# V turned in 32x32 blocks by VectorE ahead of its store, instead of by TensorE in each head

## The chip, the core and the metric

One core of a Trainium2 chip runs the whole program once. The engines are TensorE (PE, with its weight loads PEld), VectorE (DVE), ScalarE (ACT), GpSimd (POOL) and SyncE (SP); SP, ACT and POOL also issue DMAs. The metric is the device time of one execution in microseconds (us); lower is better. Arithmetic is in float32, and most products are made of three matmuls (high part by high part and the two cross terms) on operands split into a high and a low part.

## The reference

One decoder layer over 1024 tokens of width 2048. An RMS norm of the input goes into one projection with 8192 columns: queries, keys, values and gates of 8 stick-breaking heads (head width 128) and 8 differential heads (two q/k pairs of width 64, values of 128). Cut to what matters here:

```
hn = rmsnorm(h, norm_mix_g)
sb_q, sb_k, sb_v, sb_g, df_q, df_k, df_v, df_g = split(hn @ w_in)
sb_out = stick_breaking_attention(sb_q, sb_k, sb_v)          # w @ v, tokens contracted
df_out = rmsnorm(differential_attention(rope(df_q), rope(df_k), df_v, lam), subln_g) * (1 - lambda_init)
mixed  = concat(sb_out * silu(sb_g), df_out * silu(df_g))
h = h + mixed @ w_out
h = h + sigmoid(rmsnorm(h, norm_ple_g) @ w_ple_gate) * (p @ w_ple_proj)
out = rmsnorm(h, norm_final_g)
```

## The kernel before

All activations are kept transposed: features on the 128 partitions, tokens along the free axis. The 1024 tokens are two halves of 512; half 1 comes first in the attention. A tile is mostly 128x512.

The program has four stages.

**1. V and gates (to about 620 us).** The columns of values and gates are computed with a seven-product scheme on 2x2 blocks (the products are called A11, A12, S1, S2, S3, S4 and A22 after their operand). Class `Seven` runs it: `prod` writes the twelve matmuls of one product and then calls `step`, which is one *slot*: it splits one weight operand for later products (`whigh` on ACT, `wlow` on DVE, with the differences T1 to T4 on DVE), runs what `soon` holds for this slot, and takes from the queue `xq`. A *unit* u (0 to 15) is one head's V and gate. In phase 0 a unit is S2, A22 of the unit before, S1, S4 of the unit before, S3; in phase 1 it is A11, A22 of the unit before, S2, S4 of the unit before, A12, S1, S3. An opening computes A11 and A12 of phase 0 for all units first (`outer` and `evict` for units 0 to 7, a loop for 8 to 15). Results leave PSUM through DVE (`u2`, `u3`, sums into the tiles `hc`) or, where nothing is to be added, through an ACT copy (`evict`, and `second_result` for A12), and `vput` stores them to `vg_d`, with addition in DRAM after the first. S2 and S3 accumulate in one PSUM bank b: A22 of the same unit adds to it after S3, so `u3` (b + s1) must have read it before; the line is L1255. Four tiles with the tag "f" take the outgoing results in turn.

**2. Heads (about 620 to 1650 us).** For each half and each of 16 heads (the differential ones first), `unit` writes the 192 matmuls of the q and k projection, and between every three matmuls `side.tick()` runs what is due of the attention of the head before: tables of tick numbers (`SVG`, `VGD`, `SBT`, `TT`, ...) give the place of each step. `load_vg` loads the head's V and gate (tiles `vf`, `gf`) on SP, `normed` multiplies them by the tokens' RMS factor `rstd`, and `values` turns V: four TensorE transposes of 128x128 into the PSUM tile `vps`, since the product with the attention weights contracts tokens; then ACT casts the high part and DVE makes the low part.

```
vps = pp.tile([P, 4, P], F32, name="vps", tag="t")
for j in range(4):
    T.transpose(vps[:, j, :], vg[0][:, j * P:(j + 1) * P], ident)
```

**3. Output projection (about 1660 to 1985 us)**, again by `Seven` (`op`), 8 units in 2 phases. In phase 1 `sums` forms row combinations of the new h for the next stage, in two steps `one` and `two` put on `soon` in following slots. `u3` stands there too (L1912). **4. The embedding gate (from about 1985 us)**, 8 units, by `gprod`; `gate_loads` issues the loads of an operand and puts its splits on `xq` some slots on; `plew` (L1851) casts the embedding weights, `ple` multiplies with them.

The order of PE, DVE and ACT is that of the code: each runs its instructions in the order in which they are written, and every wait is a semaphore. POOL's and SP's orders follow from the planner. DMAs on SP are issued in order.

Of the kernel before, what the change touches and what calls it, by code (L numbers as in the profile page):

```python
# [13 lines left out]
F32 = mybir.dt.float32  # L14
# [3 lines left out]
ALU = mybir.AluOpType  # L18
AX = mybir.AxisListType

P = 128
# [4 lines left out]
H = 8  # L26
# [13 lines left out]
LV = ((2.5, 2.5), (1, 2))  # L40
# [30 lines left out]
def _body(ctx, nc, tc, ap):  # L71
    PSUM = bass.MemoryType.PSUM
    const = ctx.enter_context(tc.tile_pool(name="const", bufs=1))
# [20 lines left out]
    G.memset(eps5, SUB_EPS)  # L94
    lsum = const.tile([P, 2], F32, name="lsum", tag="lsum")
    lam = const.tile([P, 1], F32, name="lam", tag="lam")
    qzs = {}
    nqz = [0]

# [206 lines left out]
        G.dma_start(S4, t, accum_op=ALU.add)  # L306


    def attention(at, pz, half, hd, q, qz, K, KL, VV, sg, vg, state):

        sb = hd < H
# [143 lines left out]
        def values():  # L455

            assert "v" in state
            vps = pp.tile([P, 4, P], F32, name="vps", tag="t")
            for j in range(4):
                T.transpose(vps[:, j, :], vg[0][:, j * P:(j + 1) * P], ident)  # L460
            v = at.tile([P, 2, 4, P], F32R, name="v", tag="v")
            side.later(1 if sb else LV[half][0], lambda: A.copy(v[:, 0], vps))

            def low():
                V.tensor_tensor(v[:, 1], vps, v[:, 0].bitcast(F32), op=ALU.subtract)
                VV.insert(0, v)
                if half == 1:
                    G.dma_start(v_d[hd], v.rearrange("p a b c -> p (a b c)"))

            side.later(2 if sb else LV[half][1], low)  # L470

        def turn(pr, g):

# [149 lines left out]
    with tc.tile_pool(name="at", bufs=2) as at, ExitStack() as banks:  # L623
# [26 lines left out]
        def ftile():  # L650
            return ev.tile([P, HALF], F32, name="hc", tag="f", bufs=4)
# [254 lines left out]
        def combined(i):  # L906
# [25 lines left out]

            return {nm: partial(part, nm) for nm in ("S1", "S2", "S3", "S4", "A22")}

        def vput(o, ph, hf, blk, u):
            G.dma_start(vg_d[hf, blk, u], o, **(dict(accum_op=ALU.add) if ph else {}))  # L936

# [267 lines left out]
        for u in range(H, 2 * H, 2):  # L1205
            pair = []
            for nm in ("A11", "A12"):
                for j in range(2):
                    if nm == "A11":
                        pair.append(pp.tile([P, HALF], F32, name="pa", tag="acc", bufs=2))  # L1210
                    prod(u + j, 0, nm, pair[j], nm == "A11")
                    o = ftile()
                    A.copy(o, pair[j])
                    if nm == "A11":
                        G.dma_start(vgpart_d[u + j], o)
                    else:
                        vput(o, 0, 1, 0, u + j)
        prev = None
        for ph in range(2):
            for u in range(2 * H):  # L1220
# [74 lines left out]
                consts_late()  # L1295

        side.add([(4, norms)])
        X0 = {}

        early = {}  # L1300
# [59 lines left out]
        def gate_operand(nm, i, eng):  # L1360

            hi, lo = op.places(GPLACE[nm][i], "g" + nm)
            src = {"A11": h_d[1, i], "A12": h_d[1, i + 8], "A22": h_d[0, i + 8]}.get(nm)
            if src is None:
                src = hcomb_d[SUMS.index(nm), i]
            gain = {"A11": i, "A12": i + 8, "A22": i + 8, "S3": i}.get(nm)
            if gain is not None:
                gain = gvec[:, 1, gain:gain + 1]
            if nm == "A12":
                with tc.issue_after(op.loaded.ins):  # L1370
                    eng.dma_start(lo.bitcast(F32), src)
# [116 lines left out]
        for half in (1, 0):  # L1488
# [5 lines left out]
            for hd in (ORDER0, ORDER1)[half]:  # L1494
# [10 lines left out]
                def load_vg(vg=vg, hd=hd, half=half):  # L1505
                    for i in range(2):
                        vg.append(f32t(("vf", "gf")[i]) if hd < H else ev.tile([P, HALF], F32, name=("vf", "gf")[i], tag="xt", bufs=4))
                        with tc.issue_after(lastw[0].ins):
                            nc.sync.dma_start(vg[i], vg_d[half, i, hd])
# [49 lines left out]
                if sb:  # L1559
# [18 lines left out]
                    def normed(i, vg=vg, rstd=rstd, state=state):  # L1578
                        V.tensor_tensor(vg[i], vg[i], rstd, op=ALU.mult)
# [8 lines left out]
                else:  # L1588
# [19 lines left out]
                    def turned(c, fs=fs):  # L1608
                        f, sw = [t.bitcast(F32) for t in fs[c]]
                        V.tensor_tensor(sw, sw, cs[:, 1, :], op=ALU.mult)  # L1610
                        V.tensor_tensor(f, f, sw, op=ALU.add)
# [24 lines left out]
                        if c:  # L1636
                            store_k()

                    def normed(i, vg=vg, rstd=rstd, state=state):
                        V.tensor_tensor(vg[i], vg[i], rstd, op=ALU.mult)  # L1640
# [166 lines left out]
        def rest_of(st_, first):  # L1807

            u, ph, b, c, s1, u2, hq = st_
            nm, o_, t, hf, ch = ("A22", b, s1, 0, u) if first else ("S4", c, u2, 1, u + 8)  # L1810
            prod(u, ph, nm, o_, False)
            o = ftile()
            V.tensor_tensor(o, o_, t, op=ALU.add)
            put(o, ph, hf, ch)
            if ph == 1:
                hrows[u, hf] = o
                if not first:
                    lag = {6: 10, 7: 7}.get(u, 1)
                    op.soon.extend((op.slot + lag + i, fn) for i, fn in enumerate(sums(u, hq, hrows.pop((u, 0)), hrows.pop((u, 1)))))

        praws = []

# [599 lines left out]
```

## Time and profile before

| | us |
|---|---|
| median of three runs (2359.6 to 2361.01) | 2360.39 |
| the profiled execution | 2361.19 |
| its span, first to last instruction | 2359.4 |
| PE busy in the span | 2317.2 |
| DVE busy | 1789.8 |
| ACT busy | 1189.0 |

The profile is of one execution. A group's row gives busy time and the mean of one instruction; a wait's row gives who waited for whom, in total, how often and the longest. A row of the timeline gives start, length, engine, line, operation, output and input. Line numbers (L460) are those of the kernel before.

### The profile page before, as it was taken

What the parts mean: (1) busy time and instruction counts of PE and PEld (TensorE: products, weight loads), DVE (VectorE), ACT (ScalarE), POOL (GpSimd) and SP (SyncE); (2) the same over time, 40 slices, a digit from 0 to 9 for tenths busy, and PEclk for the clock granted to TensorE, in tenths of its full rate; (3) what the DMA queues carried; (4) which work ended last, traced back from release to release, by engine and by line L of the source; (5) the groups of instructions that cost most, each with busy time, mean ns of one, the idle gap of its engine ahead of it and who ended that gap; (6) DMA issues with size and microseconds to landing.
All of it is one profiled execution on the core that took longest, in us unless ns stands there. A gap on an engine that the chain in (4) does not pass through costs nothing.

```text
span 2359.4 us, 32445 instructions
## 1 busy us (share of the span) xinstructions
PE 2317.2 (98%) x11096; PEld 1928.3 (82%) x11096; DVE 1789.8 (76%) x3123; ACT 1189.0 (50%) x2214; POOL 327.3 (14%) x480
## 2 busy tenths in 40 slices
PE   9999999999999999999999999999999999999997
PEld 7888888888888878887888888888878878788886
DVE  7489676666677787777888876767887877788778
ACT  6334243333367775445676764445633435533544
POOL 2211112332200000000001011011121232000000
PEclk9999999999999999999999999999999999999998
DMA  7699589999977788787656566677888778898666
GB/s 260 225 313 344 170 255 281 293 278 271 303 246 252 246 266 299 256 263 245 204 182 199 165 190 215 203 214 238 213 211 215 242 229 269 291 326 292 243 227 217
DMA packets 252725, 581.02 MB, mean 246 GB/s; under 512 B 28496, under 2 KB 41040, under 8 KB 252560
## 3 DMA queue, kind: packets, MB, share of 16 engines
q1 hardware_dynamic: 177952, 394.34, 49.7%
q0 software_dynamic: 55312, 149.71, 24.2%
q10 hardware_dynamic: 19296, 34.90, 4.3%
q8 instruction: 87, 1.43, 0.3%
q14 instruction: 78, 0.64, 0.1%
HBM read 373.32 MB, written 213.91 MB: 249 GB/s over the span
## 4 chain that ended last, share of the span: by engine, by line
PE 71%; DVE 12%; ACT 7%; DMA 6%; issue 3%; SPq 0%; ACTq 0%; DVEq 0%
PE acc L263 7%; PE acc L261 7%; PE acc L262 7%; PE pbc L708 6%; PE pbc L710 6%; PE pbc L709 6%; PE pa L708 2%; PE pa L710 2%; PE pa L709 2%; PE tp L480 2%; DMA wraw<-w_out 2%; PE pb L708 1%; PE pb L710 1%; PE pb L709 1%; PE pb L1941 1%
## 5 line engine op out<-in xcount | busy, mean ns | idle before, releaser
L799 ACT CAST wpr<-T 128x512 fp32r<-128x512 f32 x208 | 125.3, 621 | 440.3 <-DVE T L764 360.4
L261 PE MATMUL acc<-xh,whi 128*128 128x512 f32 x768 | 315.0, 410 | 0.0
L263 PE MATMUL acc<-xh,wlo 128*128 128x512 f32 x768 | 302.5, 394 | 1.5 <-DMA wlo<-wlo_d 1.4
L262 PE MATMUL acc<-xl,whi 128*128 128x512 f32 x768 | 301.0, 392 | 0.0
L263 PEld LDWEIGHTS acc<-xh,wlo 128*128 128x128 f32 x768 | 144.5, 188 | 36.2 <-DMA wlo<-wlo_d 3.6
L262 PEld LDWEIGHTS acc<-xl,whi 128*128 128x128 f32 x768 | 145.4, 189 | 24.0
L261 PEld LDWEIGHTS acc<-xh,whi 128*128 128x128 f32 x768 | 145.0, 189 | 23.4 <-DVE qk L1567 0.2
L799 ACT CAST wpr<-wraw 128x512 fp32r<-128x512 f32 x144 | 88.6, 618 | 146.9 <-DMA wraw<-w_vg 40.2
L813 DVE TENSOR_TENSOR wpr<-T,wpr 128x512 fp32r<-128x512 f32 x208 | 145.8, 701 | 9.2 <-ACT wpr L799 6.8
L936 POOL DMA_DIRECT2D vg_d<-hc x120 | 86.8, 724 | 328.4 <-DVE hc L1181 187.9
L503 DVE TENSOR_TENSOR awl<-tp,awh 128x256 fp32r<-128x256 f32 (+1 forms) x160 | 92.5, 578 | 42.8 <-ACT awh L498 42.2
L498 ACT CAST awh<-tp 128x256 fp32r<-128x256 f32 (+1 forms) x160 | 80.6, 504 | 82.6 <-PE tp L480 76.3
L813 DVE TENSOR_TENSOR wpr<-wraw,wpr 128x512 fp32r<-128x512 f32 x144 | 97.7, 686 | 23.5 <-ACT wpr L799 23.5
L321 DVE CUSTOM_DVE_ANT_0 z<-z,masks 128x512 f32<-128x512 f32 (+7 forms) x128 | 97.1, 769 | 23.0 <-PE z L341 14.0
L708 PE MATMUL pbc<-cS,wpr 128*128 128x512 f32 x288 | 112.0, 389 | 0.0
L709 PE MATMUL pbc<-cS,wpr 128*128 128x512 f32 x288 | 112.0, 389 | 0.0
L710 PE MATMUL pbc<-cS,wpr 128*128 128x512 f32 x288 | 112.0, 389 | 0.0
L373 DVE TENSOR_TENSOR_SCAN st<-pt 128x511 f32<-128x511 f32 (+3 forms) x64 | 86.7, 1354 | 27.2 <-ACT pt L366 26.8
L366 ACT ACTIVATE pt<-z 128x512 f32<-128x512 f32 (+3 forms) x64 | 41.8, 653 | 76.6 <-DVE z L349 74.6
L528 PE MATMUL av<-awl,v 128*128 128x256 f32 x256 | 73.4, 287 | 1.7 <-DVE awl L503 1.7
L526 PE MATMUL av<-awh,v 128*128 128x256 f32 x256 | 72.0, 281 | 0.7 <-ACT awh L498 0.7
L527 PE MATMUL av<-awh,v 128*128 128x256 f32 x256 | 72.2, 282 | 0.0
(589 smaller groups left out, 6816.5 us busy)
## 6 DMA issues: line engine op xcount, KB each, us to landing
wlo<-wlo_d SPq DMA_DIRECT2D x94, 512.0 KB, 5.2
whi<-whi_d SPq DMA_DIRECT2D x74, 512.0 KB, 4.1
wraw<-w_vg SPq DMA_DIRECT2D x129, 256.0 KB, 4.8
vg_d<-hc POOLq DMA_DIRECT2D x120, 256.0 KB, 5.7
wraw<-w_in SPq DMA_DIRECT2D x54, 512.0 KB, 5.3
wraw<-w_gate SPq DMA_DIRECT2D x92, 256.0 KB, 4.9
wraw<-w_out SPq DMA_DIRECT2D x72, 256.0 KB, 4.6
wlo_d<-wlo SPq DMA_DIRECT2D x34, 512.0 KB, 3.4
```

Source lines behind the costliest of these rows:

```text
L261: T.matmul(acc[c], hi[:, k2, kh, c, :], xh, start=first, stop=False)
L262: T.matmul(acc[c], hi[:, k2, kh, c, :], xl, start=False, stop=False)
L263: T.matmul(acc[c], lo[:, k2, kh, c, :], xh, start=False, stop=last)
L321: V.tensor_tensor_reduce(z, z, mwide[:, 0:n], -DF_SCALE, 3.0e38, ALU.add, ALU.min, mx)
L373: V.tensor_tensor_scan(st[:, off + 1:nkey], pt[:, off:nkey - 1], pt[:, off:nkey - 1], initial=1.0, op0=ALU.mult, op1=ALU.bypass)
L503: V.tensor_tensor(wl[:, o, :], tp[:, o, :], wh[:, o, :].bitcast(F32), op=ALU.subtract)
L708: T.matmul(o, wh[:, w], xh, start=start and k == 0, stop=False, skip_group_check=True)
L709: T.matmul(o, wh[:, w], xl, start=False, stop=False, skip_group_check=True)
L710: T.matmul(o, wl[:, w], xh, start=False, stop=k == 3, skip_group_check=True)
L799: A.copy(t[:, 0], src)
L813: V.tensor_tensor(t[:, 1], src, t[:, 0].bitcast(F32), op=ALU.subtract)
L936: G.dma_start(vg_d[hf, blk, u], o, **(dict(accum_op=ALU.add) if ph else {}))
```

## The change

V is turned before it is stored. VectorE's transpose works on blocks of 32x32: `vturn` turns the sixteen blocks of each 128-token group of a 128x512 tile and writes them sorted by the place of the 32 tokens in their group of 128. Each head's load then puts the blocks where they belong: four DMAs, one for each 32 partitions, gather runs of 128 elements from the four partition groups. The head's V thus arrives with tokens on the partitions.

```
+    def blocks(t):
+        return t.rearrange("p (b k j) -> p b k j", b=4, k=4)
...
+        def vturn(o, src):
+            V.transpose(blocks(o).rearrange("p b k j -> p k b j"), blocks(src))
...
         def values():
-            vps = pp.tile([P, 4, P], F32, name="vps", tag="t")
-            for j in range(4):
-                T.transpose(vps[:, j, :], vg[0][:, j * P:(j + 1) * P], ident)
             v = at.tile([P, 2, 4, P], F32R, name="v", tag="v")
-            side.later(1 if sb else LV[half][0], lambda: A.copy(v[:, 0], vps))
+            hi, lo = [v[:, i].rearrange("p k (b j) -> p b k j", b=4) for i in range(2)]
+            raw = blocks(vg[0])
+            A.copy(hi, raw)
             def low():
-                V.tensor_tensor(v[:, 1], vps, v[:, 0].bitcast(F32), op=ALU.subtract)
+                V.tensor_tensor(lo, raw, hi.bitcast(F32), op=ALU.subtract)
...
-            side.later(2 if sb else LV[half][1], low)
+            side.later(1, low)
...
         def evict(n, u):
-            if u in (3, 5) and n == 3:
+            if n > 3:
+                vturn(o, aa[u])
+            elif u in (3, 5):
...
         def rest_of(st_, first):
             V.tensor_tensor(o, o_, t, op=ALU.add)
-            vput(o, ph, hf, blk, u)
+            if not first:
+                return vput(o, ph, hf, blk, u)
+            def turned():
+                v = ftile()
+                vturn(v, o)
+                vput(v, ph, hf, blk, u)
+            if ph == 1 and u == 2 * H - 1:
+                turned()
+            else:
+                gv.soon.append((gv.slot + 2, turned))
...
                 def second_result():
                     prod(u, ph, "A12", a, False)
                     o = ftile()
-                    A.copy(o, a)
+                    vturn(o, a)
...
+        def columns(hf):
+            ps = pp.tile([P, 4, P], F32, name="rps", tag="t")
+            for j in range(4):
+                T.transpose(ps[:, j, :], rstds[hf][:, j * P:(j + 1) * P], ident)
+            side.later(1, lambda: A.copy(rcol[:, hf, :], ps[:, :, 0]))
+        side.add([(20, partial(columns, 1)), (24, partial(columns, 0))])
...
-                            nc.sync.dma_start(vg[i], vg_d[half, i, hd])
+                            if i:
+                                nc.sync.dma_start(vg[i], vg_d[half, i, hd])
+                            for a in range(0 if i else 4):
+                                rows = slice(32 * a, 32 * a + 32)
+                                nc.sync.dma_start(vg[i][rows].rearrange("p (b e) -> p b e", b=4), vg_d[half, i, hd].rearrange("(b p) (a e) -> a p b e", b=4, a=4)[a])
```

The loop of the opening for units 8 to 15 gets `vturn` in place of the ACT copy at A12 in the same way. Since tokens are now on the partitions, `normed` multiplies V by a factor per partition and token group: `columns` turns the two rows of factors once into `rcol`, with eight TensorE transposes in the first head. Two places of the later stages move:

```
-        e = [(op.slot + (3 if nm in ("A11", "A12") else 2), gate_operand(nm, i0 + j, eng)) for j in range(n)]
+        e = [(op.slot + (3 if nm in ("A11", "A12") or eng is A and (nm, i0) == ("S2", 0) else 2), gate_operand(nm, i0 + j, eng)) for j in range(n)]
...
-                    op.soon.extend((op.slot + lag + i, fn) for i, fn in enumerate(sums(...)))
+                    op.soon.extend((op.slot + lag + (1 + (lag == 1)) * i, fn) for i, fn in enumerate(sums(...)))
```

What stands in the queues, at three places. On DVE, the end of the first unit of phase 1 in the V stage, before (wpr is a weight operand, T a difference of weight blocks, hc a result on its way out):

```order
L1236 TENSOR_TENSOR u_2895<-pbc,s_2826 128x512
L813 TENSOR_TENSOR wpr<-T_2782,wpr 128x512
L1181 TENSOR_TENSOR hc<-pbc,u_2716 128x512
L813 TENSOR_TENSOR wpr<-wraw,wpr 128x512
L690 TENSOR_TENSOR cS4l<-cS4l,cS4h 128x512 x2
L764 TENSOR_TENSOR T_2961<-wraw 128x512
L764 TENSOR_TENSOR T_2964<-wraw,T_2961 128x512
L813 TENSOR_TENSOR wpr<-wraw,wpr 128x512
L690 TENSOR_TENSOR cS4l<-cS4l,cS4h 128x512 x2
L1255 TENSOR_TENSOR u_2973<-pbc,s_2826 128x512
```

and the same piece now:

```order
L1256 TENSOR_TENSOR u_2925<-pbc,s_2857 128x512
L816 TENSOR_TENSOR wpr<-T_2810,wpr 128x512
L939 STREAM_TRANSPOSE hc<-hc 128x4x4x32
L1189 TENSOR_TENSOR hc<-pbc,u_2745 128x512
L816 TENSOR_TENSOR wpr<-wraw,wpr 128x512
L693 TENSOR_TENSOR cS4l<-cS4l,cS4h 128x512 x2
L939 STREAM_TRANSPOSE hc<-pa 128x4x4x32
L767 TENSOR_TENSOR T_2994<-wraw 128x512
L767 TENSOR_TENSOR T_2997<-wraw,T_2994 128x512
L816 TENSOR_TENSOR wpr<-wraw,wpr 128x512
L693 TENSOR_TENSOR cS4l<-cS4l,cS4h 128x512 x2
L1275 TENSOR_TENSOR u_3006<-pbc,s_2857 128x512
```

Two block transposes have come in ahead of u3 (L1255, now L1275): that of the A22 result two slots earlier, and that of A12, which reads its bank. On PE, in the second head of half 1, before:

```order
L263 MATMUL acc_5697<-xh_5159,wlo 128x512
L460 MATMUL vps<-ident,vf 128x128 x4
L261 MATMUL acc_5697<-xh_5162,whi 128x512
L262 MATMUL acc_5697<-xl_5163,whi 128x512
L263 MATMUL acc_5697<-xh_5162,wlo 128x512
```

and now:

```order
L264 MATMUL acc_5775<-xh_5222,wlo 128x512
L262 MATMUL acc_5775<-xh_5225,whi 128x512
L263 MATMUL acc_5775<-xl_5226,whi 128x512
L264 MATMUL acc_5775<-xh_5225,wlo 128x512
L262 MATMUL acc_5776<-xh_5216,whi 128x512
```

The four transposes are gone and nothing stands in their place. On DVE in phase 1 of the output projection, before (hq and hc are rows of the new h, hr the old ones):

```order
L1798 SCALAR_TENSOR_TENSOR hq<-hq,gneg 128x512
L1800 SCALAR_TENSOR_TENSOR hc<-hc,gneg,hq 128x512
L1912 TENSOR_TENSOR u_17915<-pbc,s_17780 128x512
L813 TENSOR_TENSOR wpr<-T_17906,wpr 128x512
L1914 TENSOR_TENSOR u_17915<-u_17915,hr 128x512
L1919 TENSOR_TENSOR hq<-pbc,u_17915 128x512
```

and now:

```order
L1952 TENSOR_TENSOR u_17924<-pbc,s_17793 128x512
L816 TENSOR_TENSOR wpr<-T_17919,wpr 128x512
L1838 SCALAR_TENSOR_TENSOR hq<-hq,gneg 128x512
L1840 SCALAR_TENSOR_TENSOR hc<-hc,gneg,hq 128x512
L1954 TENSOR_TENSOR u_17924<-u_17924,hr 128x512
L1959 TENSOR_TENSOR hq<-pbc,u_17924 128x512
```

The two combinations stand behind u3 and the weight remainder, in six of the eight units. In the gate stage the casts of the first four S2 operands on ACT stand behind one more cast of `plew`, one weight cast and one sigmoid.

More of the change, by code (lines that the diff above doesn't have):

```diff
@@ L96, in _body @@
     lam = const.tile([P, 1], F32, name="lam", tag="lam")
+    rcol = const.tile([P, 2, 4], F32, name="rcol", tag="rcol")
     qzs = {}
@@ L1212, in _body @@
                     o = ftile()
-                    A.copy(o, pair[j])
                     if nm == "A11":
+                        A.copy(o, pair[j])
                         G.dma_start(vgpart_d[u + j], o)
                     else:
+                        vturn(o, pair[j])
                         vput(o, 0, 1, 0, u + j)
@@ L1576, in taken, with normed @@
                         side.later(2, low)
-                    def normed(i, vg=vg, rstd=rstd, state=state):
-                        V.tensor_tensor(vg[i], vg[i], rstd, op=ALU.mult)
+                    def normed(i, vg=vg, rstd=rstd, state=state, half=half):
+                        if i:
+                            V.tensor_tensor(vg[i], vg[i], rstd, op=ALU.mult)
+                        else:
+                            r = rcol[:, half, :].rearrange("p (b k j) -> p b k j", b=1, j=1)
+                            V.tensor_tensor(blocks(vg[i]), blocks(vg[i]), r.broadcast_to([P, 4, 4, 32]), op=ALU.mult)
                         state.add("v")
@@ L1637, in spread, with normed @@
                             store_k()
-                    def normed(i, vg=vg, rstd=rstd, state=state):
-                        V.tensor_tensor(vg[i], vg[i], rstd, op=ALU.mult)
+                    def normed(i, vg=vg, rstd=rstd, state=state, half=half):
+                        if i:
+                            V.tensor_tensor(vg[i], vg[i], rstd, op=ALU.mult)
+                        else:
+                            r = rcol[:, half, :].rearrange("p (b k j) -> p b k j", b=1, j=1)
+                            V.tensor_tensor(blocks(vg[i]), blocks(vg[i]), r.broadcast_to([P, 4, 4, 32]), op=ALU.mult)
                         state.add("v")
@@ L1818, in rest_of @@
                     lag = {6: 10, 7: 7}.get(u, 1)
-                    op.soon.extend((op.slot + lag + i, fn) for i, fn in enumerate(sums(u, hq, hrows.pop((u, 0)), hrows.pop((u, 1)))))
+                    op.soon.extend((op.slot + lag + (1 + (lag == 1)) * i, fn) for i, fn in enumerate(sums(u, hq, hrows.pop((u, 0)), hrows.pop((u, 1)))))
         praws = []
```

## The prediction

> **What bounds the kernel now.** I read the page's engine shares first, then the time by stage, then who waits for whom on TensorE (PE), then single steps in the timeline.
>
> ```profile
> PE 2317.2 (98%) x11096; PEld 1928.3 (82%) x11096; DVE 1789.8 (76%) x3123; ACT 1189.0 (50%) x2214; POOL 327.3 (14%) x480
> ```
>
> PE is busy for 2317.2 of 2359.4 us: only 42 us are without a matmul. Whatever leaves PE's queue is gained unless another engine then holds PE up. The stages (start:end, length, busy us of PE, PEld, DVE, ACT, POOL, granted clock, DMA share, GB/s):
>
> ```profile
> 103.64:198.84 95.20, 95.20 (x421) 78.83 (x420) 83.89 (x135) 36.04 (x63) 20.04 (x37) 1.00 0.92 314
> 198.84:226.36 27.52, 27.52 (x123) 22.77 (x122) 26.03 (x42) 12.50 (x22) 2.74 (x6) 1.00 0.99 358
> 226.36:294.04 67.68, 67.68 (x300) 56.05 (x299) 48.27 (x79) 19.16 (x32) 8.69 (x16) 1.00 0.56 182
> 294.04:329.52 35.48, 35.32 (x156) 28.90 (x154) 29.05 (x46) 17.56 (x31) 4.15 (x7) 1.00 0.70 220
> 329.52:610.80 281.28, 280.53 (x1237) 232.28 (x1238) 185.00 (x268) 102.00 (x160) 86.30 (x121) 1.00 1.00 283
> ...
> 640.00:900.00 260.00, 254.22 (x1267) 211.60 (x1266) 201.48 (x490) 179.98 (x418) 16.85 (x29) 1.00 0.75 255
> 900.00:1200.00 300.00, 293.56 (x1490) 246.66 (x1490) 232.09 (x438) 165.18 (x325) 20.32 (x31) 0.99 0.73 244
> ```
>
> The first five rows are the V and gate stage (the first four its phase 0, the fifth its phase 1): PE has no gap, DVE is at 88%, 95%, 71%, 82% and 66%, ACT at half or less. The last two are heads of attention: PE 98%, DVE 77%. The clock is full throughout. PE's waits (us in total, times, longest):
>
> ```profile
> PE pbc L708 <- DVE u L1912: 3.5, 4, 1.5
> ...
> PE z L1859 <- ACT pwhl L1851: 1.5, 1, 1.5
> ...
> PE pbc L708 <- DVE u L1255: 0.9, 1, 0.9
> ```
>
> None is a wait for the V transposes. They cost PE its own time.
>
> **PE loses 128 transposes (values).** The timeline at one group (start, length):
>
> ```profile
> 656.87 0.39 PE L262 MATMUL acc<-xl,whi 128*128 128x512 f32 x1
> 657.10 0.39 PE L263 MATMUL acc<-xh,wlo 128*128 128x512 f32 x1
> 657.33 0.60 PE L460 MATMUL vps<-ident,vf 128*128 128x128 f32 x4
> 657.69 0.48 PE L261 MATMUL acc<-xh,whi 128*128 128x512 f32 x1
> 658.00 0.40 PE L262 MATMUL acc<-xl,whi 128*128 128x512 f32 x1
> ...
> L460 PE MATMUL vps<-ident,vf 128*128 128x128 f32 x128 | 19.2, 272 | 0.0
> ```
>
> A matmul of 512 columns starts every 0.23 us. Without the four, L261 would start at 657.33 and L262 at 657.56; it starts at 658.00. So a group costs 0.44 us, and 32 groups 14.1 us, all on the path. The 272 ns of the last row is the time through the array, not what one takes from the queue (four end after 0.60).
>
> [...]
>
> Added: two groups of four (columns), 0.9 us. They stand at ticks 20 and 24 of the first head; the rotary table reads one half's factors at tick 20 too, so they are made by then, and I see no wait.
>
> **DVE gains 64 block transposes.** 32 replace ACT copies (16 in the opening, 16 at A12 of phase 1), 32 come on top (A22: one per unit in both phases). No such operation is in the trace. The nearest row is the lane shuffle of the same tile from PSUM:
>
> ```profile
> L1606 DVE STREAM_SHUFFLE sw<-acc 128x512 f32<-128x512 f32 x32 | 23.6, 736 | 0.0
> L373 DVE TENSOR_TENSOR_SCAN st<-pt 128x511 f32<-128x511 f32 (+3 forms) x64 | 86.7, 1354 | 27.2 <-ACT pt L366 26.8
> ```
>
> I take 0.74 us (the scan's 1.35 is the upper end), 47 us in all. A unit of phase 0 is five products of twelve matmuls, 13.6 us (95.2 / 7): 83.89 + 7 x 0.74 = 89.1 of 95.2 in the first seven units, 26.03 + 1.5 = 27.5 of 27.5 in the next two, then slack again. Phase 1 has 185.0 + 30 x 0.74 = 207 of 281. What PE would wait for is u3, read from the bank before A22 may add to it:
>
> ```profile
> 198.84 0.69 DVE L1255 TENSOR_TENSOR u<-pb,s 128x512 f32<-128x512 f32 x1 [0.81 <-PE pb L710]
> 213.21 0.68 DVE L1255 TENSOR_TENSOR u<-pbc,s 128x512 f32<-128x512 f32 x1
> 226.36 0.68 DVE L1255 TENSOR_TENSOR u<-pbc,s 128x512 f32<-128x512 f32 x1
> ...
> 329.52 0.69 DVE L1255 TENSOR_TENSOR u<-pbc,s 128x512 f32<-128x512 f32 x1
> ...
> 330.27 0.50 PE L708 MATMUL pbc<-cA,wpr 128*128 128x512 f32 x1 [0.90 <-DVE u L1255]
> ```
>
> At 198.84 it starts as S3 ends. The next S3 ends at 212.44, so u3 at 213.21 is 0.77 late; at 226.36, 0.32. One transpose more per unit makes that about 1.5 and 1.8. PE follows u3's start by 0.75 (329.52 to 330.27), and A22 is due one product (13.6 / 5 = 2.72) after S3's end: 1.8 + 0.75 = 2.55, just no stall. At 330 there is none to spare: 0.90 is waited already, and up to three transposes come into that stretch, 0 to 2.2 us. I take +1.5 for the stage (0 to 5, the upper end with 1.35 a piece).
>
> [...]
>
> The ring of four output tiles is filled once more per unit, and the turned A22 tile is stored two products later, so POOL's stores change order. A tile is free once its store has landed:
>
> ```profile
> vg_d<-hc POOLq DMA_DIRECT2D x120, 256.0 KB, 5.7
> ```
>
> Four fills in 13.6 us leave each tile more than twice that; cost 0, and up to 1 in the opening, where stores and products share the ring (inside the 5 above).
>
> ACT loses 32 copies, where it idles. The V cast and its remainder keep their counts and are no longer behind PE; they stand a row or two earlier, and K's remainder then comes after them. That, and the V factor by column, I put at 0 (under 0.7 of DVE, hidden by PE's products).
>
> **V's load is four DMAs of 512 B pieces, not one of 2 KB rows.** On the SP queue:
>
> ```profile
> L1509 SPq DMA_DIRECT2D vf<-vg_d x32: 319/424/1072, 632.2 to 1628.3; - x32
> ...
>   DMA vf<-vg_d: 0.2, 1
> ...
> L1845 SPq DMA_DIRECT2D pw<-w_pp x32: 545/556/953, 1990.4 to 2305.6; - x32
> ...
> vf<-vg_d SPq DMA_DIRECT2D x32, 256.0 KB, 5.7
> ...
> pw<-w_pp SPq DMA_DIRECT2D x32, 128.0 KB, 4.8
> ...
> 877.71 0.77 SPq L1509 DMA_DIRECT2D vf<-vg_d  x1
> ...
> 884.04 0.69 DVE L1579 TENSOR_TENSOR vf<-vf,ssa 128x512 f32<-128x512 f32 x1 [0.19 <-DMA vf<-vg_d]
> ```
>
> The pw load is the nearest: 512 B pieces, 256 of them, land 4.8 us after an issue of 0.56. Four issues of 0.42 to 0.56 put the last piece 1.3 to 1.7 later and its landing at about 6.1 to 6.5 instead of 5.7. The gate load and the next weights are that much later on SP (96 more issues in all). DVE waits for V once in 32 heads, 0.2 us: at 884.04, 6.3 us after the issue, in a stick-breaking head of the first half run. Those eight heads have 4 ticks from load to use, all others 6 to 19.5. There DVE, and behind it the gate factor, the weight remainders and the scan, may wait 0.3 to 0.8 a head, some 4 us; with DVE at 77% I take a third, 1.2, on PE (0 to 4).
>
> **Row combinations later (output stage).** Before:
>
> ```profile
> 1918.10 0.39 PE L708 MATMUL pa<-cA11h,wpr 128*128 128x512 f32 x1
> 1918.15 0.74 DVE L1798 SCALAR_TENSOR_TENSOR hq<-hq,gneg 128x512 f32<-128x512 f32 x1
> 1918.93 0.75 DVE L1800 SCALAR_TENSOR_TENSOR hc<-hc,gneg,hq 128x512 f32<-128x512 f32 x1
> 1919.60 0.69 DVE L1912 TENSOR_TENSOR u<-pbc,s 128x512 f32<-128x512 f32 x1
> 1920.34 0.50 PE L708 MATMUL pbc<-cA,wpr 128*128 128x512 f32 x1 [1.40 <-DVE u L1912]
> ```
>
> The two go behind u3, which then starts 1.45 earlier. The four waits (3.5, and 0.16 each of modelled tail over the 0.23 step, 4.1) go but for some 0.3. Next in line is the weight chain of that unit, so I take -3.0 (0 to -4.1).
>
> **S2 splits a slot later.** ACT's two casts no longer stand ahead of pwhl:
>
> ```profile
> 2028.77 1.27 ACT L684 CAST cgS<-cgS 128x512 fp32r<-128x512 f32 x2 [0.93 <-DMA cgS<-hcomb_d]
> 2029.94 0.40 ACT L1851 CAST pwhl<-pw 128x256 fp32r<-128x256 f32 x1
> 2030.40 0.50 PE L1859 MATMUL z<-ph,pwhl 128*128 128x512 f32 x1 [1.49 <-ACT pwhl L1851]
> ```
>
> That frees pwhl by two casts and the 0.93: -1.5 (0 to -1.65).
>
> **Sum.** The profiled execution took 2361.19 us (0.80 above the median of the three). 2361.2 - 14.1 + 0.9 + 1.5 + 1.2 - 3.0 - 1.5 = 2346.2. The bounds: 2361.2 - 14.1 + 0.9 - 4.1 - 1.65 = 2342 and, with nothing gained late, 2361.2 - 13.2 + 5 + 4 = 2357, not all at once.
>
> **Rivals.**
> - *Block transposes far dearer (slower).* Phase 0 has 226 - 187 = 39 us of idle DVE for its 16, 2.4 each, phase 1 96 for 32, 3.0 each. Beyond that each us lands on PE: at 3.5 us, 16 x 1.1 + 32 x 0.5 = 34, so 2380; it ends slower from about 3.1 us. The shuffle and the scan speak against it. 0.03.
> - *DVE late for u3 in each unit of phase 0* (the transpose waits for tiles still being stored, or costs 1.3): 16 x 0.5 + 2 more, 2354. For it, the 95% in two units; against it, the 12% that DVE idles in the seven before and 29% in the five behind. 0.10.
> - *V comes late in both halves:* 2 us of DVE in 16 heads, a quarter on PE, 8 us: 2353. For it, four issues on a queue that carries every weight; against it, 6 to 19.5 ticks of lead and the one wait of 0.2. 0.07.
> - *Heads paced by DVE and ACT, not PE:* the 14 us turn into waits, about 2358. DVE at 77% and only some 12 us of PE gaps in 560 speak against it. 0.05.
> - *Transposes cost 272 ns each:* 2325. 0.04.
>
> **How the numbers follow.** The forecast has 0.71, so I predict 2346. 2339 to 2354 takes in the bounds, the second and third rival, and some 3 us below for ACT's and PSUM's relief, which I can't price. A measurement tells 0.2% (4.7 us) from no change: faster 0.90 (the forecast, most of the second and third rival, the fifth), same 0.07, slower 0.03.
>
> **What would show it.** PE's busy time lower by some 13 us with no vps rows; block transposes of about 0.74 us; PE waits on L1255's successor up by no more than 2 us, on L1912's near zero, none for pwhl at 2030. I am wrong if PE's waits in the V stage grow past 6 us, if vf's DVE waits pass 10 us, or if the head stages don't shorten.

## The result, and the profile after

The changed kernel is slower: 2365.95 us (median of 18 runs) against 2360.24 for the kernel before, timed beside it, a ratio of 1.0023 [1.0015, 1.0030]. 2346 was predicted. Its profiled execution took 2364.57 us (span 2362.5) against 2361.19, so the traces below show 3.4 of the 5.7 us. One run of e15 (5572 us) and one of the kernel before (6994 us) were slow runs and are left out of all medians and ratios below.

Busy time by engine, on the page of the changed kernel:

```profile
PE 2307.4 (98%) x10976; PEld 1919.0 (81%) x10976; DVE 1826.3 (77%) x3187; ACT 1170.6 (50%) x2184; POOL 329.1 (14%) x480
```

PE has 120 instructions fewer and is busy 9.8 us less, but the part of the span in which it isn't busy grew from 42 to 55 us, and the 9.8 hold some matmuls that ran at half clock: one started every 0.43 us there (907 to 910) instead of every 0.23, and the granted clock was 0.50 for 13.7 us up to 2300, for 3.4 in the kernel before. PE's waits, after (total, times, longest):

```profile
PE acc L264 <- DMA wlo<-wlo_d: 6.5, 7, 1.6
PE pbc L711 <- DVE u L1952: 4.8, 5, 2.1
PE acc L262 <- DVE qk L1599: 4.3, 2, 3.2
...
PE z L344 <- ACT et L401: 3.8, 7, 0.7
...
PE z L340 <- ACT k L1607: 2.8, 1, 2.8
...
PE acc L262 <- DVE sw L1642: 1.6, 1, 1.6
...
PE pbc L711 <- DVE hq L1959: 1.3, 1, 1.3
...
PE pbc L711 <- DVE u L1275: 0.8, 1, 0.8
```

L1952 is u3 of the output stage (L1912 before, 3.5), L1599 and L1607 are the first steps of q and k (2.8 and 1.5 before), L1275 is u3 of the V stage (0.9 before). Before, wlo had 1.4 and et 0.2:

```profile
PE acc L263 <- DMA wlo<-wlo_d: 1.4, 2, 0.9
...
PE z L340 <- ACT et L397: 0.2, 1, 0.2
```

Only the wait for pwhl at 2030 went, as forecast. Where the time went is seen by setting the same matmul of both timelines side by side: how much later (or earlier, negative) than in the kernel before it starts, in us. e6, e7 and e14 are experiments below.

| at (us, before) | what lies ahead of it | after | e6 | e7 | e14 |
|---|---|---|---|---|---|
| 609 | V and gate stage | 0.45 | 0.08 | 0.70 | 0.33 |
| 640 | the two rps groups | 1.45 | 0.08 | 1.69 | 0.33 |
| 843 | differential heads, half 1 | -2.09 | -1.95 | -1.87 | -3.28 |
| 1090 | stick-breaking heads, half 1 | 0.32 | -1.67 | -1.42 | -6.33 |
| 1411 | differential heads, half 0 | 3.98 | -2.25 | -1.93 | -7.56 |
| 1645 | stick-breaking heads, half 0 | 0.79 | -5.12 | -5.49 | -10.43 |
| 1984 | output projection | 5.20 | -4.61 | -6.01 | -11.51 |
| 2040 | the first S2 splits | 2.96 | -5.51 | -6.08 | -12.42 |
| 2340 | rest of the gate stage | 3.51 | -5.62 | -5.04 | -11.34 |

In the changed kernel the gain comes as forecast where seven groups of transposes lie between 640 and 843 (-3.5) and seven between 1411 and 1645 (-3.2). Three stretches lose it: the middle of the heads (843 to 1090: +2.4), the differential heads of half 0 (to 1411: +3.7) and the output projection (+4.4). The prediction had named heads that do not get shorter as a sign of being wrong: from 640 to 1645 they are only 0.7 us shorter.

### The profile page after: what moved, and what is told of

Read it like the earlier page. It is cut to its first block, busy times and chain, and to the rows that moved or that the text cites. A ratio compares the mean times of both kernels' runs of the same rounds, so it can differ in the third digit from the quotient of the medians.

```text
span 2362.5 us, 32448 instructions
## 1 busy us (share of the span) xinstructions
PE 2307.4 (98%) x10976; PEld 1919.0 (81%) x10976; DVE 1826.3 (77%) x3187; ACT 1170.6 (50%) x2184; POOL 329.1 (14%) x480
## 4 chain that ended last, share of the span: by engine, by line
PE 70%; DVE 12%; DMA 8%; ACT 8%; issue 2%; SPq 0%; ACTq 0%; DVEq 0%
PE pbc L711 6%; PE pbc L713 6%; PE pbc L712 6%; PE acc L264 6%; PE acc L262 6%; PE acc L263 6%; DMA wlo<-wlo_d 3%; PE pa L713 2%; PE pa L711 2%; PE pa L712 2%; PE tp L483 2%; DMA wraw<-w_out 2%; PE pb L711 1%; PE pb L713 1%; PE pb L712 1%
```

## The experiments

Each was timed beside the kernel before on one chip, in four groups (the median of the kernel before was 2361.8 to 2361.9 in each). The changed kernel was timed in another group, where the kernel before had 2360.24. A difference from the kernel before can therefore be taken from the medians; one from the changed kernel is better taken from the ratios, and comes out about 1.5 us larger so. A single trace can differ from the median by up to 7 us (e12), so sizes are taken from medians and ratios, and mechanisms from traces.

| run | median us | ratio to before |
|---|---|---|
| e1 | 2361.53 | 0.9996 [0.9985, 1.0006] |
| e2 | 2362.38 | 1.0004 [0.9995, 1.0013] |
| e3 | 2363.86 | 1.0012 [1.0002, 1.0021] |
| e4 | 2362.14 | 1.0004 [0.9994, 1.0013] |
| e5 | 2365.92 | 1.0016 [1.0006, 1.0026] |
| e6 | 2355.29 | 0.9971 [0.9961, 0.9980] |
| e7 | 2359.37 | 0.9990 [0.9982, 0.9999] |
| e8 | 2360.17 | 0.9990 [0.9981, 0.9999] |
| e9 | 2364.41 | 1.0011 [1.0002, 1.0021] |
| e10 | 2359.29 | 0.9988 [0.9979, 0.9998] |
| e11 | 2362.34 | 1.0003 [0.9994, 1.0013] |
| e12 | 2363.94 | 1.0008 [0.9995, 1.0020] |
| e13 | 2358.48 | 0.9990 [0.9980, 1.0000] |
| e14 | 2349.81 | 0.9946 [0.9934, 0.9957] |
| e15 | 2360.54 | 0.9990 [0.9981, 0.9999] |

### What the transposes were worth: e6, e13, e14

**e6**, the kernel before without them (V then stays unturned):

```
-            vps = pp.tile([P, 4, P], F32, name="vps", tag="t")
-            for j in range(4):
-                T.transpose(vps[:, j, :], vg[0][:, j * P:(j + 1) * P], ident)
+            vps = vg[0].rearrange("p (k j) -> p k j", k=4)
```

> The kernel before without the 128 transposes of V on TensorE, and nothing else: V's cast and remainder read the loaded tile at the ticks of before (V is then not turned). It measures what the transposes were worth. The prediction's own step (0.44 us for each of 32 groups, all on the path): 2347. Theory H (in the seven differential heads of half 0 and at two places of half 1 TensorE runs ahead into a wait that other engines end, so that there the 0.44 turns into waiting for et, qk or sw): waits for et rise from 0.2 to about 3.8, that for qk at 907 from 2.8 to 3.2, some 10 us gained at a full clock and 8 if the clock drops after the longer gap; 2350 to 2353.

Measured: -6.6 us, a smaller gain than either theory forecast, but the waits are those of theory H. Its PE waits:

```profile
PE z L340 <- ACT et L397: 4.1, 8, 0.8
PE acc L261 <- DVE qk L1565: 3.6, 2, 3.2
```

In the table of offsets, e6 gains only 0.6 between 1090 and 1411 (-1.67 to -2.25), where nine groups, eight of them of differential heads, should have brought 4.0. **e13** puts the transposes back in just these eight heads, into the combined kernel e7:

```
             raw = blocks(vg[0])
+            if not sb and half == 0:
+                spare = pp.tile([P, 4, P], F32, name="spare", tag="t")
+                for j in range(4):
+                    T.transpose(spare[:, j, :], vg[0][:, j * P:(j + 1) * P], ident)
```

> The kernel e7 (V's steps at old ticks, combinations in consecutive slots), with the four TensorE transposes of V put back in the differential heads of half 0 alone, into a spare bank that nobody reads. Theory H (there TensorE waits for et anyway): the waits for et fall from 4.1 to under 1 us and the time stays that of e7, 2359.4 within 1. The prediction's step (0.44 us a group on the path): 8 x 0.44 = 3.5 us slower, 2363.

Measured: 2358.48 against 2359.37, with the same ratio of 0.9990, and so no dearer, though a difference under some 3 us would not show in these runs. The traces are sharper: between 1090 and 1411 e7 gains 0.5 us and e13 loses 0.1, where the prediction's step would make it lose 3.5 more than e7. The wait for et is nearly gone:

```profile
PE z L344 <- ACT et L401: 0.6, 2, 0.4
```

There a score matmul waits for the exponentials to leave its PSUM tile; ACT and DVE set that time, and the four transposes stood in what is otherwise a wait of about 0.5 us.

The rest is clock: with three of PE's waits in the changed kernel, of 3.24, 2.84 and 2.08 us (ending at 906.48, 1077.87 and 1943.06), the granted clock fell to 0.50, from 906.6, 1077.3 and 1944.3 on, for 3.4, 6.8 and 3.4 us. Stretches of 1 us around the wait for qk, in the changed kernel and then one in the kernel before (start:end, length, busy us of PE, PEld, DVE, ACT, POOL, granted clock, DMA share, GB/s):

```profile
906.00:907.00 1.00, 0.52 (x2) 0.46 (x3) 0.55 (x3) 0.43 (x2) 0.42 (x1) 0.81 0.57 229
907.00:908.00 1.00, 1.00 (x4) 0.81 (x3) 0.91 (x2) 1.00 (x3) 0.00 (x0) 0.50 1.16 354
908.00:909.00 1.00, 1.00 (x3) 0.75 (x3) 1.00 (x3) 0.25 (x1) 0.00 (x0) 0.50 1.00 127
909.00:910.00 1.00, 1.00 (x4) 0.76 (x3) 0.96 (x5) 0.62 (x1) 0.00 (x0) 0.50 1.01 225
910.00:911.00 1.00, 1.00 (x6) 0.83 (x5) 1.00 (x3) 0.83 (x3) 0.06 (x1) 0.98 1.03 379
```

```profile
908.00:909.00 1.00, 1.00 (x6) 0.83 (x5) 0.91 (x2) 0.49 (x1) 0.00 (x0) 1.00 1.11 270
```

The stretch at 908 has 3 matmuls at 0.50 and 6 at 1.00. Up to 2300 us the trace of the kernel before lost 1.7 us in this way, that of the changed one 6.8, that of e6 6.8. These are single traces. The mean clock is on record for every run, and from it the loss over the whole span is on average 9.1 us in the kernel before, 11.0 in the changed one, 10.9 in e6, 10.9 in e7, 7.1 in e10 and 6.1 in e14. So half clock costs the change about 2 us, not the 5 of the two traces. **e14** is e6 with spare matmuls in the two gaps:

```
+                    if half == 1 and hd == ORDER1[10]:
+                        spare = pp.tile([P, HALF], F32, name="spare", tag="t")
+                        for i in range(12):
+                            T.matmul(spare, onesr, qzs[0][:, 0, :], start=True, stop=True)
...
+            if sb and half == 1 and hd == ORDER1[-1] and rb == 0:
+                for i in range(9):
+                    T.matmul(z[:, 0:HALF], onesr, qzs[0][:, 0, :], start=True, stop=True)
```

> The kernel before without V's transposes (e6, 2355.3), with spare matmuls in the two gaps at 905 and 1077, as in e10. Theory G: e6 lost 6.8 us to half clock after gaps, 5.1 of them (three drops) at these two places; without them 2350 to 2352. If the drops cost the end nothing, because other waits take up what is gained: 2354 to 2356.

Measured: 2349.81, 5.5 us below e6, with no stretch at half clock before 2300. At the gap:

```profile
905.00:906.00 1.00, 1.00 (x6) 0.82 (x5) 0.91 (x2) 0.40 (x1) 0.00 (x0) 1.00 1.35 244
906.00:907.00 1.00, 1.00 (x6) 0.80 (x6) 1.00 (x3) 0.24 (x1) 0.00 (x0) 1.00 0.77 117
```

So matmuls that compute nothing made the kernel faster, and the transposes are worth 9 to 10 us at full clock: 12.0 less what e14 also saves where the kernel before ran at half clock, 1.7 by the trace and 3.0 by the mean clocks.

### V's early steps and the load of wlo: e1, e2, e3, e5, e12, e8

**e1** puts V's cast and remainder back at their ticks:

```
-            A.copy(hi, raw)
+            side.later(1 if sb else LV[half][0], lambda: A.copy(hi, raw))
...
-            side.later(1, low)
+            side.later(2 if sb else LV[half][1], low)
```

> The changed kernel, but V's high cast and its remainder stand at the ticks that they had in the kernel before (1 and 2 ticks after the V step in stick-breaking heads, 2.5 and 2.5 or 1 and 2 in differential ones). With that the planner also puts POOL's load of the other half's K behind the three accumulating stores again, as before, so this undoes both. Theory A (early V work stands ahead of the exponentials and of K's and Q's steps, and TensorE waits for them): waits of z for et in half 0 fall from 3.8 us to under 1, those of acc for qk and sw in half 1 from 5.9 to about 3.4, and some 2 us of half-speed clock go; 6 to 9 us faster than the changed kernel, 2357 to 2360. Theory B (the split load of V delays the weights): waits for wlo stay at 6.5, no more than 2 us gained, 2364 or above. Theory C (POOL's order delays wlo): the wlo waits fall from 6.5 to about 1.4 as well.

Measured: 2361.53, 6.4 us below the changed kernel by the ratios (4.4 by the medians). But the wait for et stays (3.9) and those for qk and sw fall to 4.7 only: theory A had the wrong place. What fell is the wait for wlo, from 6.5 to 3.1; no theory had that number.

**e5** restores POOL's order alone, **e12** the remainder alone, **e2** the one-DMA load in the changed kernel, **e3** is the split load in the kernel before:

```
e5:  lastcomb[0] = G.dma_start(S4, t, accum_op=ALU.add)
     with tc.issue_after((lastcomb[0] or lastw[0]).ins): G.dma_start(k2..., k_d[hd])
e12: side.later(2 if sb else LV[half][1], low)      # A.copy(hi, raw) stays early
e2:  nc.sync.dma_start(vg[i], vg_d[half, i, hd])    # for both i
e3:  the change's load_vg in the kernel before
```

> The changed kernel, but POOL's load of the other half's K is held behind the three accumulating stores of the head before, as in the kernel before; V's cast and remainder stay early. It parts what the first run undid together. Theory C (of the 6.4 us most is POOL's order): waits for wlo fall from 6.5 to about 3.3, as in the kernel before with the split load, and the time by 3 to 4.5 us, 2361.5 to 2363. Theory A (it is V's early steps): less than 1.5 us gained, 2364.5 or above, with the waits in half 1 unchanged in both cases.

> The changed kernel with V's remainder back at its old tick and the cast on ScalarE still early. POOL's order stays that of the changed kernel. Theory A1 (it is the cast: it stands ahead of the exponentials, the sub-norm's sg waits behind the reciprocal of their sums on VectorE, and the accumulating stores go out 0.5 us nearer to wlo's load): sg to wlo stays at 3.8 us, wlo waits stay at 5 to 8, 2364 to 2366. Theory A2 (it is the remainder on VectorE): sg to wlo is 4.3 us again, wlo waits at 2 to 3, 2360 to 2362.

> The changed kernel, but each head's V comes by one DMA of 2 KB rows instead of four of 512-byte pieces (V's blocks are then not in their places, which no time depends on). The order on every other queue stays that of the changed kernel. Theory B (the split load delays wlo): waits for wlo fall from 6.5 to about 1.5, 4 to 6 us faster than the changed kernel, 2360 to 2362. Theories A and C (V's early steps, POOL's order): the waits for wlo and et stay within 1 us, 2364 to 2367.

> The kernel before, but each head's V comes by the four DMAs of 512-byte pieces (V's blocks are then permuted); TensorE still turns V, and POOL's order is that of before. Theory B: wlo waits rise from 1.4 to about 6, 4 to 6 us slower than before, 2364 to 2366. Theories A and C: within 1.5 us of before, 2360 to 2362; the prediction's own term for this was +1.2.

PE's waits for wlo in e1, e5, e12, e2 and e3, in this order:

```profile
PE acc L264 <- DMA wlo<-wlo_d: 3.1, 5, 1.2
```

```profile
PE acc L264 <- DMA wlo<-wlo_d: 8.0, 6, 2.3
```

```profile
PE acc L264 <- DMA wlo<-wlo_d: 5.2, 6, 1.4
```

```profile
PE acc L264 <- DMA wlo<-wlo_d: 4.1, 6, 1.7
```

```profile
PE acc L263 <- DMA wlo<-wlo_d: 3.3, 5, 1.1
```

In e5 the waits for wlo do not fall (8.0 against 6.5), and its gain is 1.7 us by the ratios and none by the medians, so theory C falls. By the ratios e12 gains 3.5 us and e2 4.5 (2.0 and 3.6 by the medians); e3 loses 2.1 against the kernel before. Theory B's forecasts for e2 and e3 (waits of 1.5 and 6) came only half true, and so did those against it. Over all 17 traces two things sort the waits: with one load and the old ticks they are 0 to 2.8 us in total (five kernels); with the split load and the old ticks 1.7 to 4.1 (seven); with one load and an early cast 4.1 (e2); with both 5.2 to 8.0 (four). Both belong to the change: about 2 us for the split load (e3) and 4 to 6 for the early steps (e1), of which the remainder alone has 2.0 to 3.5 (e12), although its waits for wlo stay at 5.2, as theory A1 has it. Whether the pieces of 512 bytes or the four issues make the split load dear is not parted. Such waits also differ by some 2 us between traces of nearly the same kernel (e7, e8, e10).

How the cast could do it is read from a differential head of half 0, after and then in e1:

```profile
1238.85 0.60 ACT L465 CAST v<-vf 128x512 fp32r<-128x512 f32 x1
...
1240.37 0.16 DVE L406 RECIPROCAL l<-l 128x1 f32<-128x1 f32 x1 [0.20 <-ACT et L401]
...
1240.45 0.67 DVE L588 SCALAR_TENSOR_TENSOR sg<-sg,rsub 128x512 f32<-128x512 f32 x1
...
1242.61 0.69 DVE L591 SCALAR_TENSOR_TENSOR sg<-msqs,sg 128x512 f32<-128x512 f32 x1
1243.33 0.32 SPq L304 DMA_DIRECT2D comb_d<-sg  x1
...
1246.39 0.45 SPq L184 DMA_DIRECT2D wlo<-wlo_d  x1
...
1257.07 0.50 PE L264 MATMUL acc<-xh,wlo 128*128 128x512 f32 x1 [1.55 <-DMA wlo<-wlo_d]
```

```profile
1237.73 0.67 DVE L588 SCALAR_TENSOR_TENSOR sg<-sg,rsub 128x512 f32<-128x512 f32 x1
1239.03 0.60 ACT L465 CAST v<-vf 128x512 fp32r<-128x512 f32 x1
1239.89 0.69 DVE L591 SCALAR_TENSOR_TENSOR sg<-msqs,sg 128x512 f32<-128x512 f32 x1
...
1244.18 0.45 SPq L184 DMA_DIRECT2D wlo<-wlo_d  x1
```

With the early cast, ACT starts an exponential 0.6 us later; on DVE the reciprocal of its sums waits for it, and the head's last product sg stands behind. From sg (L591) to the weight load it is 3.78 us after, 4.29 in e1, 3.77 in e12. The four stores that sg releases and POOL's loads are thus in flight half a microsecond nearer to wlo, whose 512 KB PE still waits for 10.7 us after their issue. The distance and the waits go together in all these kernels; that the nearer stores are what delays wlo was not tried by itself.

**e8** issues V's loads 8 ticks earlier, in e7: `VGD = ((23, 37, ...` instead of 31.

> As the run before, and in the differential heads of half 0 the loads of V and gate are issued 8 ticks (about one weight piece, 9 us) earlier, ahead of the weight loads that they followed. Theory B (the 512-byte pieces, in flight with wlo, make it late): waits for wlo fall from about 3.1 to under 1.5, 1.5 to 2.5 us faster than the run before. The rival (the same bytes are in flight with another weight piece, which is late instead): within 1 us of it.

Measured: 2360.17 against 2359.37, and 3.7 us of waits for wlo against 1.7. Nothing gained: the rival's forecast.

### Row combinations and S2 splits: e4, e9, e11

**e4** takes the combinations back in the changed kernel, **e9** moves them alone in the kernel before (what moves is the second step of `sums`, its two DVE operations):

```
e4:  op.slot + lag + i
e9:  op.slot + lag + (1 + (lag == 1)) * i
```

> The changed kernel, but the second row combination of a unit of the output stage stands in the slot after the first again, ahead of u3. Theory L (the unit is paced by a loop: u3, weight difference T3, the load that reuses its buffer, the cast, the row of the new h, the combinations, u3; moving the combinations only shifts waiting inside it and lengthens it by 0.5 us): the stretch from 1645 to 1985 us is 2 to 4 us shorter, 2362 to 2364 in all. The rival, that the combinations later are worth their 3.0 us and something else slowed this stage: 3 us slower, 2369.

> The kernel before with the second row combination one slot later, as the change has it, and nothing else. The prediction's step: the waits for u3 go, 3.0 us faster, 2359 (from 2361.9). Theory L (a loop u3, weight difference T3, load, cast, new h, combination, u3 paces the unit; the move takes 1.45 us off its end and puts 1.88 on the way to T3): five units 0.43 us longer and the last unit 2.0 longer, since its u3 follows the weight load and not S3; 2 to 4 us slower, 2364 to 2366, and the waits for u3 stay at 3 to 5 us.

Measured: e9 is 2.6 us slower than before, e4 4.5 us faster than the changed kernel by the ratios (3.8 by the medians), both as theory L has it. u3 of the last three units in the kernel before and in the changed one, and of the last two in e9:

```profile
1940.42 0.68 DVE L1912 TENSOR_TENSOR u<-pbc,s 128x512 f32<-128x512 f32 x1
1960.00 0.68 DVE L1912 TENSOR_TENSOR u<-pbc,s 128x512 f32<-128x512 f32 x1
1974.68 0.69 DVE L1912 TENSOR_TENSOR u<-pbc,s 128x512 f32<-128x512 f32 x1 [0.80 <-PE pbc L710]
```

```profile
1942.32 0.68 DVE L1952 TENSOR_TENSOR u<-pbc,s 128x512 f32<-128x512 f32 x1
1963.48 0.68 DVE L1952 TENSOR_TENSOR u<-pbc,s 128x512 f32<-128x512 f32 x1
1980.19 0.67 DVE L1952 TENSOR_TENSOR u<-pbc,s 128x512 f32<-128x512 f32 x1
```

```profile
1967.64 0.68 DVE L1912 TENSOR_TENSOR u<-pbc,s 128x512 f32<-128x512 f32 x1
1983.31 0.69 DVE L1912 TENSOR_TENSOR u<-pbc,s 128x512 f32<-128x512 f32 x1
```

A unit is paced by a loop: u3, the weight difference T3, the load into the buffer that T3 has read, a cast on ACT that stands ahead of the scaled row, the combination, the next u3. From the issue of its load to the cast it takes 7.4 to 9.9 us in these three traces, whatever the order. Moving the second step takes 1.45 us off the end of the loop but puts 1.88 between u3 and T3 (5.49 us in the changed kernel, 3.61 before):

```profile
1898.21 0.75 DVE L1800 SCALAR_TENSOR_TENSOR hc<-hc,gneg,hq 128x512 f32<-128x512 f32 x1
...
1898.71 1.39 POOL L1404 TENSOR_TENSOR total<-total,masks 128x512 f32<-128x512 f32 x1 [2.27 <-ACT masks L1403]
...
1898.88 0.68 DVE L1912 TENSOR_TENSOR u<-pbc,s 128x512 f32<-128x512 f32 x1
...
1902.49 0.69 DVE L764 TENSOR_TENSOR T<-wraw 128x512 f32<-128x512 f32 x1
```

```profile
1900.13 0.68 DVE L1952 TENSOR_TENSOR u<-pbc,s 128x512 f32<-128x512 f32 x1
...
1901.40 1.82 POOL L1432 TENSOR_TENSOR total<-total,masks 128x512 f32<-128x512 f32 x1 [2.27 <-ACT masks L1431]
...
1902.11 1.67 DVE L1840 SCALAR_TENSOR_TENSOR hc<-hc,gneg,hq 128x512 f32<-128x512 f32 x1
...
1905.62 0.68 DVE L767 TENSOR_TENSOR T<-wraw 128x512 f32<-128x512 f32 x1
```

A part of the 1.88 is that the second operation takes 1.67 us in its new place instead of 0.75. It does so in the five units, in the changed kernel and in e9, in which it starts while an addition runs on POOL, and in no other unit of these kernels; that the addition slows it is read from this coincidence and was not tried by itself.

So PE waits as before, and the last unit, which before was free of the loop (14.68 us, u3 waiting only for PE), is caught in it: 16.71 after, 15.67 in e9.

**e11** moves the S2 splits alone: the `3 if ... eng is A and (nm, i0) == ("S2", 0)` of the diff in the kernel before.

> The kernel before with the S2 splits a slot later, and nothing else. The prediction's step: the wait of z for pwhl (1.5 us) goes, -1.5 us, 2360.4; the rival, that these loads vary and the wait is now met at another place: within 0.5 us of before.

Measured: no difference. The first pwhl is free, but four casts of splits now stand ahead of the next one, 7 us on:

```profile
2036.12 0.50 PE L1859 MATMUL z<-ph,pwhl 128*128 128x512 f32 x1 [1.66 <-ACT pwhl L1851]
```

The changed kernel's trace shows neither wait; there PE comes to this place 5 us late.

### Together: e7, e10, e15

**e7** has the edits of e1 and e4, **e10** also the spare matmuls of e14, **e15** also the old S2 slots (`3 if nm in ("A11", "A12") else 2`).

> The changed kernel with V's cast and remainder at the old ticks and the row combinations in consecutive slots again. If the two act apart: 6.4 and 4 us less than the changed kernel, 2355 to 2358, which would beat the kernel before by 2 to 5 us. If they overlap (the weight loop of the output stage waits as before whatever came ahead): 2360.

> The kernel with V's steps at the old ticks and the combinations in consecutive slots (e7), with spare matmuls on constants (12 of 512 columns before the unit that waits for qk at 905, 9 before the scores that wait for k at 1077) so that TensorE is not idle there for 3.2 and 2.7 us. Theory G (a gap of over 2 us is followed by 3.4 us at half clock, 1.71 us lost each time): the clock stays at 1.00 at 906 to 910 and at 1077 to 1080, 3.4 us faster than e7, 2356. If the drops have another cause (they come at those times whatever TensorE does), no gain, 2359.

> The kernel e10 with the S2 splits in their old slots. If moving them only shifted the wait for pwhl (3.1 us at two places in e10, 1.5 before): 1 to 1.5 us faster than e10, 2358. The prediction's step (they were worth 1.5): 1.5 slower, 2361.

e7 is 2.5 us faster than the kernel before; the two repairs overlap in part (7.8 us below the changed kernel by the ratios, where 6.4 and 4.5 would make 10.9). e10 holds the clock at both gaps (1.00 throughout) and its trace is 3.6 us further ahead than e7's at 1090, but it is no faster in the end: by 1411 all of it is lost, to waits for wlo (3.8 us against 1.7) and one stretch of 3.4 us at 0.50 (from 1368.4 on) after such a wait, of 1.8 us. In e14, with one DMA for V, the gain stays. e15 differs from e10 by less than these runs can tell. e7, e8, e10, e13 and e15 are all about 0.1% faster than the kernel before (their intervals end at 0.9998 to 1.0000) and 0.3% faster than the changed one; no order among them is shown.

## Why the prediction was wrong

By its steps, in us, with what the runs put in place of each:

| step | forecast | measured | from |
|---|---|---|---|
| 32 groups of transposes | -14.1 | -6.6 | e6 |
| columns | +0.9 | +1.0 | offsets at 609 and 640 |
| V and gate stage | +1.5 | about 0 | offset at 609 |
| V's load in four | +1.2 | +2.1 | e3 |
| V's cast and remainder early | 0 | +4.4 to +6.4 | e1 (POOL's order with it) |
| row combinations | -3.0 | +2.6 | e9 |
| S2 splits | -1.5 | +0.6 | e11 |
| sum | -15.0 | +4.1 to +6.1 | the change: +5.7 |

Each measured term is uncertain by some 2.5 us, and the sum closes within that; the +0.6 of the S2 splits is not told from 0. The terms come from different kernels and need not add up, as the overlap in e7 shows. One sum can be tried: without the early steps and the row combinations the terms make -2.9, and e7, which is that kernel, measured -2.5.

**Failed: "32 groups 14.1 us, all on the path".** The 0.44 per group is about right where nothing else stands in the way: seven groups bring 3.5 us in the changed kernel and 3.6 in e14 between 640 and 843, and 3.2 and 2.9 between 1411 and 1645. What failed is "all on the path". I read a wait of 0.2 for et as an engine with time to spare, when it was one with none: PE and ACT arrived together, and any gain on PE turned into waiting there (4.1 us in eight waits in e6). Of the 7.5 us that are missing in e6, 3.9 are waits for et, about 2 half clock and 0.8 the longer wait for qk; the rest stays open and is smaller than the uncertainty. The rival "heads paced by DVE and ACT" had 0.05 and was true for eight of the heads.

**Failed: "The clock is full throughout".** The last row quoted for that sentence says 0.99. The kernel before ran at half clock at one place:

```profile
1080.00:1081.00 1.00, 1.00 (x4) 0.80 (x3) 0.97 (x4) 0.00 (x0) 0.00 (x0) 0.65 0.99 377
1081.00:1082.00 1.00, 1.00 (x4) 0.76 (x3) 0.86 (x3) 0.98 (x3) 0.00 (x0) 0.50 1.09 410
```

That row was the sign that a gap on PE can cost more than its length: here a wait of 1.47 us (1077.03 to 1078.49) was followed by 3.4 us at 0.50, 1.7 us lost. The trace of the changed kernel has three places like it, with 6.8 us lost.

**Failed: V's cast and remainder "I put at 0".** I looked at what hides their duration, not at what stands behind the cast on ACT and at whom that releases. Putting them back gained 4.4 to 6.4 us (e1), and the waits for wlo fell from 6.5 to 3.1; by which path they delay wlo is read from one head and stays open.

**Mis-sized: V's load.** The 1.2 was for DVE waiting for vf; it waited once, 1.3 us. What came late was the next weights, in half 0, not half 1.

**Failed: "The two go behind u3, which then starts 1.45 earlier"**, with the weight chain "next in line". That chain was not next, it was already what set u3's time, and the move lengthened it: alone it costs 2.6 us (e9).

**Failed: S2 "-1.5".** The wait moved to the next pwhl behind the same casts (1.66 us in e11 instead of 1.49).

**Right:** a block transpose of 128x512 takes 0.70 us (0.74 was taken), PE's wait for u3 in the V stage stayed (0.9 before, 0.8 after), and columns cost 1.0. The 1.5 us set aside for that stage were not needed. The dear rival and the one of 272 ns are out.

```profile
L939 DVE STREAM_TRANSPOSE hc<-hc 128x512 f32<-128x512 f32 x32 | 22.5, 704 | 1.3 <-DMA vg_d<-hc 1.3
L939 DVE STREAM_TRANSPOSE hc<-pa 128x512 f32<-128x512 f32 x24 | 17.1, 711 | 13.0 <-PE pa L713 12.9
```

## What to carry to other kernels

Work taken off the busiest engine is worth its time only where nobody else arrives at the same moment (in e6 nine groups between 1090 and 1411 brought 0.6 us instead of 4.0): look for the waits that are near zero (0.2 us for et here), since they show the engines that are next, head by head. Before moving a step later or earlier, follow the loop that it stands in to its slowest part; here shifting work inside a loop that a DMA paces gained nothing and lost 2.6 us (e9). A cheap instruction put ahead of another on an engine that runs its instructions in order is priced by what stands behind it and by what that releases: V's early cast and remainder, priced at 0, cost 4.4 to 6.4 us (e1).

## What the runs showed of the hardware

Some gaps on PE come with a stretch at a granted clock of 0.50. In the 17 traces, from 60 to 2300 us, there are 36 such stretches: 32 of 3.4 us at 0.50, each a loss of 1.70 or 1.71 us, and four of twice that (after, e2, e6 and e12). A matmul of 512 columns started every 0.43 us in them instead of every 0.23 (after, 907 to 910). Of 72 gaps of 1.15 to 1.5 us 2 were followed by such a stretch, of 51 of 1.5 to 2 us 9, of 21 of 2 to 3 us 15, and of 11 over 3 us 10.

Length alone does not decide. The same wait of 2.80 us near 904 was followed by it in two kernels (e3, e9) and not in two others (before, e11); the wait of 3.2 us for qk at this place was followed by it in e1 and e7 and not in e13; in the kernel before the one stretch followed a wait of 1.47 us. So the "over 2 us" of theory G (e10) is no limit in these traces. What else decides was not tried by a run of its own.
